# An f32 trunk of two layers on one core: the first feed-forward stage of layer 1 in parts of 8, 8 and 6 rows, and the S5 tables moved

## The chip, the cores and the metric

The kernel runs on 1 core of one Trainium2 chip. The time is device microseconds of one execution; lower is better. Before the change it was 1966.65 us (median of 3 runs, 1965.75 to 1967.88).

## The reference

The input `x` is 512 tokens of 1024 floats. Two layers follow, then a last RMSNorm. Each layer is a macaron:

```python
for i in range(DEPTH):                        # DEPTH = 2
    x = x + 0.5 * swiglu(rmsnorm(x, ffn1_norm[i]), ffn1_w_in[i], ffn1_w_out[i])
    h = rmsnorm(x, mix_norm[i])
    x = x + (ssd_mixer(h, ...) if i == 0 else s5_mixer(h, ...))
    x = x + 0.5 * swiglu(rmsnorm(x, ffn2_norm[i]), ffn2_w_in[i], ffn2_w_out[i])
return rmsnorm(x, final_norm)

def swiglu(h, w_in, w_out):                   # w_in 1024 x 5632, w_out 2816 x 1024
    gate, up = jnp.split(h @ w_in, 2, axis=-1)
    return (jax.nn.silu(gate) * up) @ w_out
```

The S5 mixer is a diagonal state-space model. The kernel computes it by turning inputs and states through tables of cosines and sines (eight tables of 128 x 2 x 8 x 64 floats, `s5["t"]`), which are made from the parameters and kept in DRAM.

## The kernel before

**Stages.** The program runs `f1_0`, `ssd`, `f2_0`, `f1_1`, `s5`, `f2_1` in this order; `f1` and `f2` are the two feed-forward stages of a layer, the last figure is the layer. All data is transposed: features on the 128 partitions, the 512 tokens along the free dimension (`xT[d]`, 8 tiles).

**A feed-forward stage** (`ffn`, L789). Its 2816 inner features are 22 rows of 128. A row is one gate and one up projection over 1024 inputs, then SiLU and product. The rows go in parts (L22 `PARTS`: 8, 7, 7; L23 `LAST_PARTS`: 8, 8, 6). After each part its rows are multiplied with their slice of `w_out` into the 8 output tiles, the columns `d`, and added to `xT`. Precision is kept by splitting every operand into a high and a low fp32r half (`whi` by ScalarE, `wlo` by VectorE) and adding three products: high x high, high x low, low x high.

**Two ways to multiply.** *Plain* (`proj`, L385): 128 x 128 weights against all 512 tokens. *Block products* (class `Seven`, L394): two by two blocks by a Strassen-Winograd scheme, seven products instead of eight. A row is two column blocks of the weights, split also into pairs of input tiles, and the tokens are split in halves of 256; so a product is 4 pairs x 3 matmuls of 256 tokens (`prod`, L464), and a row has 7 x 4 x 3 = 84 of them. VectorE and the accumulating DMAs from GpSimd (L407, L408) form the sums of weights.

Rows are block products in `f1_1` and `f2_1`, and from the fourth row on in `f2_0`. The output of a part is block products only where its end `b` is at most `blocks` (L822): then `seven_in` (L604) goes on behind the last row with `Columns` (L511), two columns of `w_out` at a time, so that rows, columns and the next part's rows are one unbroken sequence on TensorE. `Acts` (L533) forms the sums of the activations that this takes, during the rows. Before, `f1_1` is called with `blocks` 8 (first part alone) and `f2_1` with 16 (first and second part). Other outputs are plain (L888 to L930): for each column, load (`fetch_w`, L369), split (`split_w`, L378: cast at L380, low at L382), 3 matmuls for each row of the part (L389 to L391), evict.

**What sets the order.** TensorE's order in these stages is the program's (`manual_schedule`). VectorE's and ScalarE's instructions marked `pin` keep the program's order among themselves; the rest, and the DMA queues of SyncE (SP) and ScalarE, are ordered by the framework's scheduler, which often puts a load ahead of its place when its buffer is free. Every queue then runs in order. Weights pass through 4 buffers (`wst`), 3 of `whi` and 3 of `wlo`.

**Work threaded in: `fill`.** `ffn` calls one entry of the list `fill` after each row (not behind the first row of a part, where no row precedes) and after each plain output column (`pop`, L797). An entry issues foreign work at that place. Three kinds matter:

- *Angles* (`s5_angles`, L1587): VectorE computes cosines and sines in six pieces, in `f2_0` at entries 8 to 13, the plain output of its first part. They are stored in DRAM (`d_a`) for later.
- *Tables* (`s5_table`, L1632): each table call `i` makes two of the eight tables, for `i` and `i + 4`. It doubles the length of a complex power table six times (w = 1 to 32), by three VectorE operations each (L1653 to L1657, issued by the helper at L1637): 18 in all, on 128 x 16 w elements. Then four stores of 256 KB go out, issued by ScalarE (L1662). In three pieces (cut at operations 12 and 16). Calls 0 and 1 stand in `f2_0` at entries 23 to 28 (plain output of its second part). Calls 2 and 3 (`s5_late_tables`, L1669, with the angles loaded back by SP at L1675) stand in `f1_1` at entries 14 to 19 (plain output of its second part).
- *Loads for S5* in `f1_1`'s last plain output (entries from `end` = 29): operators `opP` (L1734) and `opH` (L1714), inputs `U` (L1707), tables `tb` (L1721) and the first GLU weights (`res_w`, L1745). The pools for these tiles (`s5_pools`, L2359) are opened by `renew` (L809) when the last block-product columns are done. The tiles `tb` and the tables under construction share three buffers.

Of the kernel before, what the change touches and what calls it, by code (L numbers as in the profile page):

```python
# [13 lines left out]
OP = mybir.AluOpType  # L14
# [7 lines left out]
PARTS = ((0, 8), (8, 15), (15, 22))  # L22
LAST_PARTS = ((0, 8), (8, 16), (16, 22))  # L23
# [6 lines left out]
PLAIN = 3  # L30
WARM = (4, 8)
RAW = 6
STAGES = ["f1_0", "ssd", "f2_0", "f1_1", "s5", "f2_1"]


@with_exitstack
def trunk_kernel(ctx, tc, x, ffn1_norm, ffn1_w_in, ffn1_w_out, mix_norm, ffn2_norm, ffn2_w_in, ffn2_w_out,
# [3 lines left out]
    nc = tc.nc  # L41
# [97 lines left out]
    def both(*fs):  # L139
        return lambda: [f() for f in fs]  # L140
# [648 lines left out]
    def ffn(pr, w_in, w_out, nxt, fill=(), ready=(), done=(), gates=(), hp=None, tail=None, blocks=0, behind=None):  # L789

        fill, ready, done, gates = list(fill), list(ready), list(done), list(gates)
# [9 lines left out]
        with tc.tile_pool(name="ffn", bufs=2, side="right", reuse_waits="tile") as fp:  # L801
# [15 lines left out]
                        pools.append(own.enter_context(tc.tile_pool(name="acts3", bufs=2, side="right", reuse_waits="tile")))  # L817
                return f

            for a, b in LAST_PARTS if final else PARTS:  # L820
                AH, AL = [], []
                if b <= blocks:  # L822
                    acts = Acts(pr, w_out, a, b, fp)
# [468 lines left out]
    s5 = {}  # L1292
# [294 lines left out]
    def s5_angles(tp):  # L1587

        c, s = s5["turn"][:, 0], s5["turn"][:, 1]
        t, d1, den = [tp.tile([128, 64], F32, name="t_" + nm, bufs=1)[:, 0:32] for nm in ("t", "d", "n")]  # L1590
        pin = tc.keep_in_program_order

        def tt(o, a, b, op):
            pin(V.tensor_tensor(o, a, b, op=op))

        def usq(cc, ss):
            tt(t, cc, ss, OP.mult)
            tt(cc, cc, cc, OP.mult)
            tt(d1, ss, ss, OP.mult)
            tt(den, cc, d1, OP.add)  # L1600
            tt(cc, cc, d1, OP.subtract)
            pin(V.tensor_scalar(den, den, -1.0, 2.0, op0=OP.mult, op1=OP.add))
            tt(cc, cc, den, OP.mult)
            pin(V.scalar_tensor_tensor(ss, t, 2.0, den, op0=OP.mult, op1=OP.mult))

        UC = tp.tile([128, 6, 32], F32, name="t_UC", bufs=1)
        US = tp.tile([128, 2, 6, 32], F32, name="t_US", bufs=1)

        def angles():
            usq(c, s)  # L1610
            usq(c, s)
            yield
            usq(c, s)
            for j in range(6):
                pin(V.tensor_copy(UC[:, j], c))
                pin(V.tensor_scalar(US[:, 0, j], s, -1.0, None, op0=OP.mult))
                pin(V.tensor_copy(US[:, 1, j], s))
                if j < 5:
                    usq(c, s)
                if j < 4:  # L1620
                    yield
            s5["a"] = dram.tile([128, 3, 6, 32], F32, name="d_a")
            nc.scalar.dma_start(s5["a"][:, 0], UC)
            nc.scalar.dma_start(s5["a"][:, 1:3], US)
            yield

        gen = angles()
        n = lambda: next(gen)
        tile = lambda nm, shp: tp.tile(shp, F32, name="t_" + nm, bufs=2 if nm == "cs" else 1)
        return [n] * 6 + [n for i in range(2) for n in s5_table(i, tile, lambda: (UC, US))]  # L1630

    def s5_table(i, tile, ang):  # L1632

        pin = tc.keep_in_program_order

        def tt(o, a, b, op):
            pin(V.tensor_tensor(o, a, b, op=op))  # L1637

        def table():
            UC, US = ang()  # L1640
            gs = slice(i * 8, i * 8 + 8)
            cs, tb = tile("cs", [128, 2, 8, 64]), tile("tb", [128, 2, 8, 32])
            pin(V.memset(cs[:, 0, :, 0:1], 1.0))
            pin(V.memset(cs[:, 1, :, 0:1], 0.0))
            for j in range(6):
                w = 1 << j
                shp = [128, 2, 8, w]
                bR = UC[:, j, gs][:, None, :, None].to_broadcast(shp)
                bI = US[:, :, j, gs][:, :, :, None].to_broadcast(shp)
                a_ = cs[:, :, :, 0:w]  # L1650
                sw = bass.AP(tensor=cs.tensor, offset=cs.offset + 512, ap=[list(cs.ap[0]), [-512, 2], [64, 8], [1, w]])
                o, t_ = cs[:, :, :, w:2 * w], tb[:, :, :, 0:w]
                tt(o, a_, bR, OP.mult)  # L1653
                if j == 5:
                    yield
                tt(t_, sw, bI, OP.mult)
                tt(o, o, t_, OP.add)  # L1657
                if j == 3:
                    yield
            for h in range(2):  # L1660
                for e in range(2):
                    nc.scalar.dma_start(s5["t"][i + 4 * h][64 * e:64 * e + 64], cs[64 * h:64 * h + 64])  # L1662
            yield

        gen = table()
        n = lambda: next(gen)
        return [n] * 3

    def s5_late_tables():  # L1669
        ang = {}  # L1670

        def load():
            for nm, a, b in (("UC", 0, 1), ("US", 1, 3)):
                t_ = s5["op"].tile([128, b - a, 6, 32], F32, tag="U", name="t" + nm, bufs=4)
                nc.sync.dma_start(t_, s5["a"][:, a:b])  # L1675
                ang[nm] = t_
            ang["tb"] = s5["op"].tile([128, 2, 8, 32], F32, tag="U", name="ttb", bufs=4)

        def tile(nm, shp):
            return s5["op"].tile(shp, F32, tag="tb", name="tcs", bufs=3) if nm == "cs" else ang["tb"]  # L1680

        return [load] + [n for i in range(2, 4) for n in s5_table(i, tile, lambda: (ang["UC"][:, 0], ang["US"]))]

    def s5_sink(d, g):

# [629 lines left out]
    for i, s in enumerate(stages[:-1]):  # L2315
        pr, prep = prep, prep_for(stages[i + 1])
        nxt = prep
        if s == "ssd":
            with tc.manual_schedule(engines=MAN):
                ssd(pr, nxt)  # L2320
        elif s == "s5":
            with tc.manual_schedule(engines=MAN):
                s5_stage(pr, nxt)
            op_es.close()
        else:
            L = int(s[-1])
            wi, wo = (ffn1_w_in, ffn1_w_out) if s[:2] == "f1" else (ffn2_w_in, ffn2_w_out)
            if s in s5_pre[:1]:
                with ExitStack() as third:

                    def tail():
                        pre_es.close()
                        hx.append(third.enter_context(tc.tile_pool(name="hx0", bufs=6, reuse_waits="tile")))
                        return third.enter_context(tc.tile_pool(name="h10", bufs=2, reuse_waits="tile"))

                    ffn(pr, wi[L], wo[L], nxt, fill=pre0, ready=ready, done=done, gates=[first_gate], tail=tail)
                    hx.clear()
            elif s in s5_pre:
                hx.append(ctx.enter_context(tc.tile_pool(name="hx", bufs=6, reuse_waits="tile")))
                with tc.tile_pool(name="hx1", bufs=2) as hp, tc.tile_pool(name="tabs", bufs=1) as tp, \  # L2340
                        tc.manual_schedule(engines=MAN):
                    tabs, fill = s5_angles(tp), [lambda: None] * 46
                    for n in (*range(8, 14), *range(23, 29)):
                        fill[n] = tabs.pop(0)
                    ffn(pr, wi[L], wo[L], nxt, fill=fill, hp=hp)
            elif stages[i + 1] == "s5":
                fill, tabs, end = [lambda: None] * 37, s5_late_tables(), 29
                for n in (9, *range(14, 20)):
                    fill[n] = tabs.pop(0)
                for j in range(2):  # L2350
                    for h in range(2):
                        fill[end + 2 * h + j] = lambda j=j, h=h: out_ops(j, h)
                for j in range(2):
                    fill[end + 2 + 2 * j] = lambda j=j: [f(j) for f in (in_h, in_u, in_t)]
                fill[end + 6] = lambda: out_ops(2, 0)
                for j in range(2 * NR):
                    fill[end + 1 + 2 * j] = lambda j=j: res_w(j)

                def s5_pools():  # L2359
                    s5["op"] = op_es.enter_context(tc.tile_pool(name="s5op", bufs=2))  # L2360
                    s5["up"] = up_es.enter_context(tc.tile_pool(name="s5u", bufs=2))

                with tc.manual_schedule(engines=MAN):
                    ffn(pr, wi[L], wo[L], nxt, fill=fill, blocks=PARTS[0][1], behind=s5_pools)
                up_es.close()
            else:
                turns = [lambda: None] * 14
                turns += [both(*[lambda d=d: fin_turn(d) for d in ds]) for ds in ((0, 1), (2, 3), (4, 5), (6,), (7,))]
                with tc.manual_schedule(engines=MAN):
                    ffn(pr, wi[L], wo[L], nxt, fill=turns, blocks=LAST_PARTS[1][1], behind=fin_open)  # L2370
# [29 lines left out]
```

## Time and profile before

| | |
|---|---|
| median of 3 runs | 1966.65 us |
| profiled execution | 1966.96 us |
| its span (first to last instruction) | 1965.2 us |
| TensorE busy | 1950.6 us (99%) |
| VectorE busy | 1613.0 us (82%) |
| ScalarE busy | 1009.5 us (51%) |
| granted TensorE clock | 0.999 |
| DMA | 303.94 MB, mean 155 GB/s |

In the profile PE is TensorE's matmuls, PEld its weight loads, DVE VectorE, ACT ScalarE, POOL GpSimd, SP SyncE; a q behind the name (SPq, ACTq) is an instruction that issues a DMA from that queue. `L472` is line 472 of the kernel. A row of the order of time gives start and length in us, engine and line, the operation, what it writes and reads, how many were merged, and in brackets how long the engine was idle before and what released it. Matmuls overlap their neighbours, so the time that one costs is the distance between starts, not its own length. In `f1_1` the rows of the first part run from about 1153, its block-product columns from 1232, the rows of the second part from 1275, its plain output from 1334, the rows of the third part from 1380, and its plain output from 1444 to 1484.

### The profile page before, as it was taken

What the parts mean: (1) busy time and instruction counts of PE and PEld (TensorE: products, weight loads), DVE (VectorE), ACT (ScalarE), POOL (GpSimd) and SP (SyncE); (2) the same over time, 40 slices, a digit from 0 to 9 for tenths busy, and PEclk for the clock granted to TensorE, in tenths of its full rate; (3) what the DMA queues carried; (4) which work ended last, traced back from release to release, by engine and by line L of the source; (5) the groups of instructions that cost most, each with busy time, mean ns of one, the idle gap of its engine ahead of it and who ended that gap; (6) DMA issues with size and microseconds to landing.
All of it is one profiled execution on the core that took longest, in us unless ns stands there. A gap on an engine that the chain in (4) does not pass through costs nothing.

```text
span 1965.2 us, 34460 instructions
## 1 busy us (share of the span) xinstructions
PE 1950.6 (99%) x13365; PEld 1758.1 (89%) x13365; DVE 1613.0 (82%) x2762; ACT 1009.5 (51%) x1611; POOL 286.0 (15%) x291
## 2 busy tenths in 40 slices
PE   9999999999999999999999999999999999999998
PEld 7888899888888888898989999998998889999997
DVE  7988878688888678877888899987878669989986
ACT  5323445465665355552535566452566446556463
POOL 1000011012111110110202112220201212222220
PEclk9999999999999999999999999999999999999999
DMA  8358767334333432684868669886987548888972
GB/s 201 100 151 204 181 145 164 100 113 142 108 107 113 115 89 72 136 182 114 183 152 185 159 135 184 188 185 170 201 255 229 165 99 169 181 183 184 192 161 86
DMA packets 535683, 303.94 MB, mean 155 GB/s; under 512 B 48896, under 2 KB 521120, under 8 KB 535520
## 3 DMA queue, kind: packets, MB, share of 16 engines
q1 hardware_dynamic: 428800, 224.66, 41.2%
q0 software_dynamic: 92640, 61.05, 20.7%
q10 hardware_dynamic: 14080, 16.04, 2.7%
q8 instruction: 105, 1.72, 0.4%
q14 instruction: 58, 0.48, 0.1%
HBM read 279.84 MB, written 21.33 MB: 153 GB/s over the span
## 4 chain that ended last, share of the span: by engine, by line
PE 94%; DVE 4%; issue 1%; ACT 1%; DMA 0%; ACTq 0%; DVEq 0%
PE mm L472 41%; PE mm L389 15%; PE mm L390 15%; PE mm L391 15%; PE aux L1203 1%; PE aux L1891 1%; PE aux L1145 1%; DVE wlo L426 1%; PE aux L1195 0%; PE aux L1096 0%; PE aux L389 0%; PE aux L390 0%; PE aux L391 0%; PE aux L1127 0%; PE aux L182 0%
## 5 line engine op out<-in xcount | busy, mean ns | idle before, releaser
L380 ACT CAST whi<-wst 128x1024 fp32r<-128x1024 f32 (+2 forms) x182 | 178.2, 984 | 294.6 <-PE mm L390 176.8
L472 PE MATMUL mm<-hx,whi 128*128 128x256 f32 x1680 | 312.1, 283 | 0.3 <-ACT gt L486 0.3
L426 DVE TENSOR_TENSOR wlo<-wst,whi 128x1024 fp32r<-128x1024 f32 x158 | 193.4, 1224 | 89.1 <-ACT whi L423 85.3
L472 PEld LDWEIGHTS mm<-hx,whi 128*128 128x128 f32 x1680 | 262.4, 192 | 1.0 <-ACT gt L486 0.5
L389 PE MATMUL mm<-hH,whi 128*128 128x512 f32 x664 | 263.3, 397 | 0.0
L391 PE MATMUL mm<-hH,wlo 128*128 128x512 f32 x664 | 259.0, 390 | 0.0
L390 PE MATMUL mm<-hL,whi 128*128 128x512 f32 x664 | 258.9, 390 | 0.0
L472 PE MATMUL mm<-hx,wlo 128*128 128x256 f32 x840 | 237.8, 283 | 0.2 <-DVE wlo L426 0.2
L382 DVE TENSOR_TENSOR wlo<-wst,whi 128x1024 fp32r<-128x1024 f32 (+2 forms) x182 | 207.2, 1141 | 29.7 <-ACT whi L380 27.9
L472 PE MATMUL mm<-hH,wlo 128*128 128x256 f32 x728 | 206.7, 284 | 0.7 <-DVE wlo L426 0.5
L472 PE MATMUL mm<-hL,whi 128*128 128x256 f32 x728 | 206.2, 283 | 0.5 <-DVE hL L273 0.3
L472 PE MATMUL mm<-hH,whi 128*128 128x256 f32 x728 | 206.1, 283 | 0.0
L423 ACT CAST whi<-wst 128x1024 fp32r<-128x1024 f32 x158 | 165.0, 1045 | 41.2 <-PE mm L472 11.7
L389 PE MATMUL mm<-ah,whi 128*128 128x512 f32 x464 | 180.7, 390 | 0.0
L390 PE MATMUL mm<-al,whi 128*128 128x512 f32 x464 | 180.6, 390 | 0.0
L391 PE MATMUL mm<-ah,wlo 128*128 128x512 f32 x464 | 180.2, 389 | 0.0
L408 POOL DMA_DIRECT2D wx<-in_ffn_w_in_dram x70 | 90.0, 1302 | 521.8 <-DMA wx<-in_ffn_w_in_dram 172.0
L472 PEld LDWEIGHTS mm<-hx,wlo 128*128 128x128 f32 x840 | 161.2, 192 | 0.4 <-DVE wlo L426 0.4
L407 POOL DMA_DIRECT2D wst<-in_ffn_w_in_dram x70 | 90.0, 1286 | 474.3 <-DMA d_P<-p_ks 196.3
L391 PEld LDWEIGHTS mm<-hH,wlo 128*128 128x128 f32 x664 | 124.6, 188 | 26.6 <-issue 0.2
L389 PEld LDWEIGHTS mm<-hH,whi 128*128 128x128 f32 x664 | 124.7, 188 | 25.8 <-issue 0.9
L390 PEld LDWEIGHTS mm<-hL,whi 128*128 128x128 f32 x664 | 124.8, 188 | 25.0 <-issue 0.2
(565 smaller groups left out, 4669.5 us busy)
## 6 DMA issues: line engine op xcount, KB each, us to landing
wst<-in_ffn_w_in_dram SPq DMA_DIRECT2D x175, 512.0 KB, 4.7
wst<-in_ssd_in_proj_dram SPq DMA_DIRECT2D x48, 512.0 KB, 3.9
wst<-in_ffn_w_out_dram SPq DMA_DIRECT2D x46, 512.0 KB, 4.2
wst<-in_ffn_w_out_dram SPq DMA_DIRECT2D x48, 448.0 KB, 4.5
wst<-in_ffn_w_in_dram POOLq DMA_DIRECT2D x70, 256.0 KB, 5.4
wx<-in_ffn_w_in_dram SPq DMA_DIRECT2D x70, 256.0 KB, 3.5
wx<-in_ffn_w_in_dram POOLq DMA_DIRECT2D x70, 256.0 KB, 6.2
dec<-d_cs POOLq DMA_DIRECT2D x16, 512.0 KB, 5.3
```

The source lines that it names most:

```text
L380: S.copy(hi, st)
L382: V.tensor_tensor(lo, st, hi.bitcast(F32), op=OP.subtract)
L389: PE.matmul(ps, hi[:, k], H[k], start=first and k == 0, stop=False)
L390: PE.matmul(ps, hi[:, k], L[k], start=False, stop=False)
L391: PE.matmul(ps, lo[:, k], H[k], start=False, stop=last and k == n - 1)
L407: G.dma_start(self.half(self.wu, 0), uo, accum_op=OP.add)
L408: G.dma_start(self.x[:, 0], ue, accum_op=OP.add)
L423: self.pin(S.copy(hi, st))
L426: self.pin(V.tensor_tensor(lo[:, c], st[:, c], hi[:, c].bitcast(F32), op=OP.subtract))
L472: PE.matmul(ps, w_[:, j], b_, start=nm not in self.open, stop=False, skip_group_check=True)
L1145: PE.matmul(pst[c], st["bt"][:, c * 128:(c + 1) * 128], st["wx"][:, c], start=True, stop=True)
L1203: PE.matmul(py[e][hh * 64:(hh + 1) * 64, s], st["dtx"][:, c, k0:k0 + 64], M[:, hh, s], start=True, stop=True)
```

## The change

- `f1_1` uses `LAST_PARTS` (8, 8, 6) and is called with `blocks` 16: its second part has 8 rows and its output is block products, its third part has 6 rows with plain output. `fill` shrinks from 37 entries to 28, and its last output column pass begins at `end` = 20 instead of 29. The last stage already used these parts.
- Table call 0 of `f2_0` moves to entries 16 to 21, behind rows of its second part, and is cut in six pieces (behind operations 6, 10, 13, 15, 16 and at the end), its stores behind the last. Calls 1 and 2, in three pieces each, take entries 23 to 28. `f2_0` so makes three table calls instead of two.
- Call 3 alone stays in `f1_1`: five pieces at entries 14 to 18, behind rows of the third part, the sixth at entry 20 (first plain output column), and its four stores at entry 27 (last column), issued by SP. The angles are loaded back when `s5_pools` opens the pools, now after the columns of the second part.

```diff
+SMALL = (6, 10, 13, 15, 16)
...
-            for a, b in LAST_PARTS if final else PARTS:
+            for a, b in LAST_PARTS if blocks else PARTS:
...
-        return [n] * 6 + [n for i in range(2) for n in s5_table(i, tile, lambda: (UC, US))]
-
-    def s5_table(i, tile, ang):
+        return [n] * 6 + [n for i in range(3) for n in s5_table(i, tile, lambda: (UC, US), *[SMALL][:i < 1])]
+
+    def s5_table(i, tile, ang, cuts=(12, 16), store=None):
...
-                tt(o, a_, bR, OP.mult)
-                if j == 5:
-                    yield
-                tt(t_, sw, bI, OP.mult)
-                tt(o, o, t_, OP.add)
-                if j == 3:
-                    yield
+                for k, (d_, x, y, op) in enumerate(((o, a_, bR, OP.mult), (t_, sw, bI, OP.mult), (o, o, t_, OP.add))):
+                    tt(d_, x, y, op)
+                    if 3 * j + k + 1 in cuts:
+                        yield
+            if store:
+                yield
             for h in range(2):
                 for e in range(2):
-                    nc.scalar.dma_start(s5["t"][i + 4 * h][64 * e:64 * e + 64], cs[64 * h:64 * h + 64])
+                    (store or nc.scalar).dma_start(s5["t"][i + 4 * h][64 * e:64 * e + 64], cs[64 * h:64 * h + 64])
             yield
...
-        return [n] * 3
+        return [n] * (len(cuts) + 1 + bool(store))
...
-        return [load] + [n for i in range(2, 4) for n in s5_table(i, tile, lambda: (ang["UC"][:, 0], ang["US"]))]
+        return [load] + s5_table(3, tile, lambda: (ang["UC"][:, 0], ang["US"]), SMALL, nc.sync)
...
-                    for n in (*range(8, 14), *range(23, 29)):
+                    for n in (*range(8, 14), *range(16, 22), *range(23, 29)):
                         fill[n] = tabs.pop(0)
...
-                fill, tabs, end = [lambda: None] * 37, s5_late_tables(), 29
-                for n in (9, *range(14, 20)):
+                fill, tabs, end = [lambda: None] * 28, s5_late_tables(), 20
+                load_angles = tabs.pop(0)
+                for n in range(14, 19):
                     fill[n] = tabs.pop(0)
...
+                fill[end] = both(tabs.pop(0), fill[end])
+                fill[end + 7] = both(fill[end + 7], tabs.pop(0))
 
                 def s5_pools():
...
+                    load_angles()
 
                 with tc.manual_schedule(engines=MAN):
-                    ffn(pr, wi[L], wo[L], nxt, fill=fill, blocks=PARTS[0][1], behind=s5_pools)
+                    ffn(pr, wi[L], wo[L], nxt, fill=fill, blocks=LAST_PARTS[1][1], behind=s5_pools)
```

## The prediction

> **What bounds the kernel now.** I read the page first, then busy time by stretch, then the chain and single engines' order of time inside the stage that changes (`f1_1`).
>
> ```profile
> span 1965.2 us, 34460 instructions
> ...
> PE   1950.6 (99%) x13365; PEld 1758.1 (89%) x13365; DVE 1613.0 (82%) x2762; ACT 1009.5 (51%) x1611; POOL 286.0 (15%) x291
> ```
>
> TensorE is busy 99% of the span: the program ends when the matmuls are done. The time can fall only by matmul time or by PE's waits, and rise only by new waits. The same by stretch (after the length: PE, PEld, DVE, ACT, POOL with counts, PE clock, DMA share, GB/s):
>
> ```profile
> 930.00:980.00 50.00, 50.00 (x419) 50.00 (x418) 40.85 (x60) 29.64 (x45) 12.83 (x10) 1.00 0.90 185
> ...
> 1334.00:1380.00 46.00, 45.47 (x227) 38.48 (x226) 35.28 (x75) 11.15 (x14) 2.56 (x2) 1.00 0.72 179
> 1380.00:1444.00 64.00, 64.00 (x534) 64.00 (x533) 54.74 (x81) 37.77 (x58) 12.84 (x10) 1.00 0.87 192
> 1444.00:1454.00 10.00, 10.00 (x53) 8.51 (x52) 6.38 (x10) 3.29 (x5) 0.00 (x0) 1.00 1.09 351
> 1454.00:1484.00 30.00, 30.00 (x136) 24.85 (x135) 17.73 (x26) 21.20 (x27) 0.71 (x2) 1.00 0.80 234
> ...
> 1755.00:1865.00 110.00, 110.00 (x919) 110.00 (x918) 101.29 (x160) 63.08 (x101) 28.27 (x22) 1.00 0.90 187
> ```
>
> The first is rows of `f2_0`'s second part. Then `f1_1`: plain output of its second part (1334 to 1380, the only stretch with PE short of full), rows of the third part (to 1444), plain output of the third part, which I call the tail (to 1484). The last is `f2_1`'s second part, rows and block-product columns: the code that the change gives to `f1_1`. PE is full there for all 110 us with DVE at 92% and DMA at 0.90, so the block path feeds PE without waits. The clock is 1.00 throughout.
>
> **The change part by part.** *Matmul time.* How far apart do matmuls start? Chain, a run of 256-column block products; and from PE's order of time the first matmul of output column 2 and the last of column 7 in the tail:
>
> ```profile
> 1152.88 181.43 PE mm L472 x1512
> ```
>
> ```profile
> 1455.09 0.39 PE L389 MATMUL mm<-ah,whi 128*128 128x512 f32 x1
> ```
>
> ```profile
> 1483.42 0.40 PE L391 MATMUL mm<-ah,wlo 128*128 128x512 f32 x1
> ```
>
> 181.43/1512 is 0.120 us for 256 columns. The other two are 6 columns x 7 rows x 3 = 126 matmuls, 125 intervals: 28.33/125 = 0.2266 us for 512 columns. So half the columns cost 53%, and seven products for eight give 7/8 x 2 x 0.120/0.2266 = 93%, not 87.5%.
> - Second part, plain, 7 rows: 7 x 8 x 3 = 168 x 0.2266 = 38.1 us go.
> - Second part, block, 8 rows: 4 column pairs x 7 products x 4 pairs of rows x 3 = 336 x 0.120 = 40.3 us come.
> - Third part, 6 rows for 7: 24 x 0.2266 = 5.4 us go.
>
> All 22 rows keep their 84 matmuls. Sum: -3.2 us. By the Trainium skill (TensorE: Matmul & The Clock Gate, "Wait — 56ns, not 53.3ns?") a warm matmul takes N ÷ 2.4 GHz and 2.5 ns, 109 and 216 ns; by it the sum would be an estimated -4.7 us. The rows disagree with it for both sizes (120 and 227 ns), and they decide.
>
> *PE's waits at the seam of second and third part.* PE, then ACT:
>
> ```profile
> 1376.47 0.28 PE L472 MATMUL mm<-hH,wlo 128*128 128x256 f32 x1
> 1377.00 0.51 PE L472 MATMUL mm<-hx,whi 128*128 128x256 f32 x2 [0.26 <-ACT gt L486]
> ```
>
> ```profile
> 1378.66 0.28 PE L472 MATMUL mm<-hL,whi 128*128 128x256 f32 x1
> 1379.21 0.39 PE L472 MATMUL mm<-hH,wlo 128*128 128x256 f32 x1 [0.27 <-DVE wlo L426]
> ```
>
> ```profile
> 1372.56 3.98 ACTq L1662 DMA_DIRECT2D d_t<-tcs  x4
> 1376.58 0.37 ACT L486 COPY gt<-mm 128x256 f32<-128x256 f32 x1 [6.55 <-DMA d_t<-tcs]
> ```
>
> Starts 0.53 and 0.55 us apart instead of 0.12: 0.84 us lost. ACT issues the four stores of a table for 3.98 us and reads the PSUM bank only then, so PE waits, and `wlo` is late behind it. The change puts no table there and joins the parts through the columns, as `f2_1` does with PE full. This stall goes: -0.8. What is late next there? Nothing in the 110 us of the twin; I keep 0 to 0.5 us of doubt. Together -4.0 us: that is the whole gain on offer.
>
> *A table among matrix rows.* Three groups of DVE's table arithmetic (two tables together, 1343 to 1379), then DVE's idle place in a row of `f1_1` and of `f2_0`, then ACT in the last row of `f2_0`'s second part:
>
> ```profile
> L1637 DVE TENSOR_TENSOR tcs<-tcs,ttb 128x16 f32<-128x16 f32 (+5 forms) x12 | 4.0, 334 | 0.2
> L1637 DVE TENSOR_TENSOR tcs<-tcs,tUC 128x16 f32<-128x16 f32 (+5 forms) x12 | 4.0, 332 | 0.2
> L1637 DVE TENSOR_TENSOR ttb<-tcs,tUS 128x16 f32<-128x16 f32 (+5 forms) x12 | 3.9, 329 | 0.0
> ```
>
> ```profile
> 1402.29 1.23 DVE L426 TENSOR_TENSOR wlo<-wst,whi 128x1024 fp32r<-128x1024 f32 x1 [1.09 <-ACT whi L423]
> ```
>
> ```profile
> 982.24 1.23 DVE L426 TENSOR_TENSOR wlo<-wst,whi 128x1024 fp32r<-128x1024 f32 x1 [1.68 <-ACT whi L423]
> ```
>
> ```profile
> 992.33 0.94 ACT L380 CAST whi<-wst 128x896 fp32r<-128x896 f32 x1 [0.98 <-PE mm L472]
> 995.81 0.63 ACT L500 ACTIVATE gt<-gt 128x512 f32<-128x512 f32 x1 [2.54 <-DVE gt L499]
> ```
>
> A table is 11.9/2 = 6.0 us of DVE in 18 operations, cut into six pieces: about 1 us a row on average. Behind a piece on DVE's queue stand the low half of the q4 weights and the next row's sum, then the `wlo` of the rows above, which waits for ACT anyway, 1.68 us in `f2_0` and 1.09 us in `f1_1`. A piece of 1.0 us fits under that, so I take 0; one 0.3 us too long in each of five rows without that cover would be 1.5 us. In `f2_0`'s last row ACT issues four stores (3.98 us by the row above) and has 0.98 + 2.54 = 3.5 us idle before the Silu. What stands behind them is the cast of output column 1, which PE wants only after column 0 (18 x 0.2266) and a product (12 x 0.120), 5.5 us. I take 0; without that cover it is 0.5 us.
>
> *The tail.* It shrinks from 168 x 0.2266 + 1.4 = 39.5 to 144 x 0.2266 + 1.4 = 34.1 us, so the weights must be ready sooner. Casts and lows of columns 3 (first of the pairs) and 7, and PE's starts (the second matmul of column 3, the first of column 7):
>
> ```profile
> 1456.09 1.78 ACT L380 CAST whi<-wst 128x896 fp32r<-128x896 f32 x2
> ```
>
> ```profile
> 1473.61 0.93 ACT L380 CAST whi<-wst 128x896 fp32r<-128x896 f32 x1
> ```
>
> ```profile
> 1458.10 2.08 DVE L382 TENSOR_TENSOR wlo<-wst,whi 128x896 fp32r<-128x896 f32 x2
> ...
> 1474.57 1.09 DVE L382 TENSOR_TENSOR wlo<-wst,whi 128x896 fp32r<-128x896 f32 x1 [0.97 <-ACT whi L380]
> ```
>
> ```profile
> 1460.08 0.39 PE L390 MATMUL mm<-al,whi 128*128 128x512 f32 x1
> ```
>
> ```profile
> 1478.89 0.39 PE L389 MATMUL mm<-ah,whi 128*128 128x512 f32 x1
> ```
>
> `wlo` of column 3 is ready at about 1459.1, wanted as third matmul at 1460.3: 1.2 us to spare. Column 7: ready 1475.66, wanted 1479.34: 3.7 us. Each row less takes 3 x 0.2266 = 0.68 us off every column before: three for column 3 (-2.0 us), seven for column 7 (-4.8 us). With unchanged ready times column 3 is 0.8 and column 7 1.1 us late, and the first wait covers most of the second: 1.1 us. Now the transfers of the tail, and where the tables' stores and reads lay:
>
> ```profile
> DMA packets 15733, 10.53 MB, mean 263 GB/s; under 512 B 6127, under 2 KB 14075, under 8 KB 15731
> ...
> wst<-in_ffn_w_out_dram SPq DMA_DIRECT2D x4, 448.0 KB, 7.5
> ```
>
> ```profile
> d_t<-tcs ACTq DMA_DIRECT2D x8, 256.0 KB, 4.6
> tb<-d_t SPq DMA_DIRECT2D x2, 512.0 KB, 5.1
> ```
>
> ```profile
> 1371.74 0.34 SPq L1721 DMA_DIRECT2D tb<-d_t  x1
> ```
>
> Stores (1 MB a table) and table reads (0.5 MB each) now fall between 1344 and 1384, where DMA was 0.72 busy. After the change the last table's stores stand on SP at the last column, and the read that reuses their buffer follows them. The pool that holds these tiles opens only in the third part, so the other two reads and the angles (0.3 MB by their shapes) go into its rows, which have 0.13 of DMA time free over 64 us; that holds 1.3 MB (7 us at 192 GB/s). Behind the stores on SP's queue stand S5's first reads of `d_u`; S5 takes the tables in turn, the third after two whole turns, so that costs nothing unless the transfers themselves are late. In the tail: 8 x 64 KB less weights (-0.5), +1.0 and +0.5: 11.5 MB in 34.1 us is 338 GB/s. The fullest 10 us (351) could do that, the tail's mean (263) could not. If only the net +0.5 MB of stores and weights stands ahead of the last weights, at 330 GB/s, that is 1.6 us more: 2.7 us lateness in all. I take the middle of 1.1 and 2.7: +1.9 us.
>
> Sum: -3.2 - 0.8 + 1.9 = -2.1 us. The profiled execution was 1966.96 us, 1.8 us around its span and 0.3 over the median of 1966.65, to which I apply the sum: **1964.5 us**.
>
> **The rivals.**
> 1. *All of the gain arrives* (-4.0 and up to 0.5 more from restarts after the two stalls: 1962.4). It needs the tail's weights to come earlier than in the old order. For it: the rows up to 1444 leave 0.13 of DMA time free and could start them; `f2_1` has no stall in its rows. Against: 1.2 us to spare at column 3.
> 2. *The tail stays as long as its data* (39.5 us): 5.4 us of waits, -4.0 + 5.4 = +1.4, 1968.1. For it: DMA at 1.09 in its first 10 us. Against: over its other 30 us DMA is at 0.80.
> 3. *Transfers moved into the tail make it DMA-bound: slower.* At the old mean of 263 GB/s 11.5 MB take 43.7 us, 9.6 us over 34.1: +5.6, 1972.3. It is slower by over 0.2% if the tail runs under 11.5 MB/(34.1 + 7.9 us) = 274 GB/s. For it: every store and read goes through the 16 engines that also bring the weights. Against: that mean holds 30 us at 234 GB/s in which DMA was not full (0.80). By the Trainium skill (Trainium Kernel Development and Optimization, "Key Constraints") transfers issued from SP, ACT and POOL share the same 16 engines and another issuer saves only issue time; that is this rival's ground, and the trace so far agrees only in that ACT's own 3.98 us go.
>
> That the change does something else than it says can be left out: `f2_1` runs the same loop.
>
> **How the numbers follow.** About 0.2% (3.9 us) is what a measurement here can tell from no change. My forecast (between -0.5 and -3.9) has 0.45, rival 1 0.27, rival 2 0.14, rival 3 0.14. Only rival 1 is faster by over 0.2%: 0.27; forecast and rival 2 are within: 0.59; rival 3 slower: 0.14. The range runs from 1961.6 (rival 1 with its doubt) to 1970.0 (half of rival 3's loss); what is left out is the outer half of rival 3 and a little below. The likeliest case alone: 1962.8 to 1966.2.
>
> **What the changed profile would show.** Right: 168 fewer + 24 fewer plain matmuls and 336 more block products in `f1_1`; no PE wait at the seam of second and third part, no table stores on ACT there; PE full in `f2_0`'s second part; the tail some 36 us long with waits for `wlo` or `whi` of columns 3 and 7. Wrong: PE short of full in `f2_0`'s rows or in the third part's rows (pieces too long, reads too many), a tail of 34 us without waits (rival 1), of 39 us or more (rivals 2 and 3), or S5's first turn waiting for a table.

## The result and the profile after

The changed kernel took 1978.43 us (median of 6 runs, 1977.25 to 1981.17); the kernel before, 1967.01 (6 runs, 1965.75 to 1968.29). The ratio is 1.0059 [1.0046, 1.0071]: 11.4 us slower, where 2 us faster was forecast, and outside the range. The profiled execution of the changed kernel took 1981.17 us, its span is 14.0 us longer than that of before. It is the longest of the six: the mean granted clock is 0.995 in it and in the next (1978.95 us), and 0.996 to 0.997 in the other four, so less of them ran at the slow clock that is shown below. The sums from this trace are therefore larger than the difference of the medians. Medians here are of all runs; the ratios leave out three runs of the last series that took 2204 us or more, one of them of the experiment with one more cut alone.

The page after:

```profile
span 1979.2 us, 34886 instructions
...
PE 1953.9 (99%) x13509; PEld 1767.7 (89%) x13509; DVE 1641.1 (83%) x2816; ACT 1022.5 (52%) x1642; POOL 296.4 (15%) x299
...
L473 PE MATMUL mm<-hx,whi 128*128 128x256 f32 x1680 | 313.4, 284 | 6.8 <-ACT gt L489 6.8
```

There are 144 more matmuls, as worked out (336 - 192). PE is still busy 99%: 7 us of idle do not show in a share. They show in the last column of the group: 6.8 us of waiting for one ScalarE copy, L489; before, this group waited 0.3 in all. (Lines up to about L1640 have moved by one: L472 is now L473.) By stretch, first the place where PE is short, last the rows of `f2_0` that the prediction showed:

```profile
985.00:990.00 5.00, 5.00 (x44) 5.00 (x44) 4.73 (x7) 3.99 (x6) 0.00 (x0) 1.00 0.44 86
990.00:995.00 5.00, 0.98 (x9) 0.77 (x7) 2.63 (x5) 0.05 (x1) 1.28 (x1) 0.85 0.92 227
995.00:1000.00 5.00, 2.26 (x10) 2.26 (x11) 0.00 (x0) 0.66 (x2) 0.00 (x0) 0.50 1.12 254
1000.00:1005.00 5.00, 5.00 (x24) 4.66 (x23) 2.89 (x4) 1.16 (x2) 0.00 (x0) 0.63 0.34 112
930.00:980.00 50.00, 50.00 (x419) 50.00 (x418) 44.28 (x77) 29.60 (x45) 12.82 (x10) 1.00 0.90 185
```

PE works 0.98 of 5 us, then 2.26, from there on at a clock of 0.50 to 0.63 (third figure from the end). This is `f2_0`'s last row before the plain output. ScalarE's order of time there, before and after:

```profile
989.38 0.62 ACT L423 CAST wh<-wst 128x512 fp32r<-128x512 f32 x1
989.89 0.37 ACT L488 COPY gt<-mm 128x256 f32<-128x256 f32 x1
990.96 0.38 ACT L491 ACTIVATE up<-mm 128x256 f32<-128x256 f32 x1 [0.70 <-PE mm L472]
```

```profile
989.43 0.61 ACT L424 CAST wh<-wst 128x512 fp32r<-128x512 f32 x1
992.09 5.19 ACTq L1662 DMA_DIRECT2D d_t<-t_cs  x4
997.32 0.37 ACT L489 COPY gt<-mm 128x256 f32<-128x256 f32 x1 [7.27 <-issue]
997.59 0.39 ACT L492 ACTIVATE up<-mm 128x256 f32<-128x256 f32 x1
1000.55 0.94 ACT L381 CAST whi<-wst 128x896 fp32r<-128x896 f32 x1 [2.57 <-PE mm L473]
```

After the cast of `wh` the copy came at once. Now the four stores of the table stand between them. VectorE's and PE's order of time after:

```profile
990.65 0.68 DVE L1638 TENSOR_TENSOR t_tb<-t_cs,t_US 128x512 f32<-128x512 f32 x1
991.37 0.69 DVE L1638 TENSOR_TENSOR t_cs<-t_cs,t_tb 128x512 f32<-128x512 f32 x1
991.98 0.68 DVE L427 TENSOR_TENSOR wl<-wst,wh 128x512 fp32r<-128x512 f32 x1
```

```profile
990.70 0.28 PE L473 MATMUL mm<-h,wlo 128*128 128x256 f32 x1
997.74 0.80 PE L473 MATMUL mm<-hx,whi 128*128 128x256 f32 x2 [6.76 <-ACT gt L489]
998.34 0.41 PE L473 MATMUL mm<-hx,wlo 128*128 128x256 f32 x1
998.55 0.63 PE L473 MATMUL mm<-hx,whi 128*128 128x256 f32 x2
998.98 0.41 PE L473 MATMUL mm<-hx,wlo 128*128 128x256 f32 x1
```

This reads as one sum. PE's next matmul was due at 990.82 (0.12 behind the last one) and starts at 997.74, 6.9 us late: 1.3 until the table's last operation ends (992.06) and the stores may start, 5.2 for their issue, 0.4 for the copy. Then the matmuls are 0.215 us apart (998.55 to 998.98 holds two) instead of 0.120: in the trace the granted clock is 0.5 from 993.5 us for 10.2 us, so 6.0 us of work run at that pace after the idle time, which loses 6.0 x (1 - 0.120/0.215) = 2.7. Together 9.6; from 995 to 1037 us of the old trace, each matmul comes 9.7 us later than there.

Following one matmul against its twin in the old trace through the rest of the program gives the whole 14.0:

| place | us against before |
|---|---|
| `f2_0`, last row of the second part and what follows it | +9.8 |
| `f1_1`, from 1280 to the end of its tail | -2.1 |
| opening of S5 (3.9 of it by the first matmul of L1805) | +6.3 |

In sum, `f1_1` did what was forecast. Its stretches (second part's columns, third part's rows, start and rest of the tail):

```profile
1340.00:1386.00 46.00, 46.00 (x385) 46.00 (x385) 42.73 (x70) 25.55 (x43) 12.44 (x10) 1.00 0.87 180
1386.00:1452.00 66.00, 65.62 (x546) 65.41 (x545) 62.15 (x104) 36.79 (x57) 13.23 (x11) 1.00 0.89 199
1452.00:1462.00 10.00, 10.00 (x67) 9.18 (x67) 7.96 (x14) 4.46 (x9) 0.00 (x0) 1.00 0.91 287
1462.00:1492.00 30.00, 29.20 (x131) 23.65 (x130) 18.64 (x28) 19.47 (x27) 1.20 (x2) 1.00 0.92 274
```

and PE's waits from 1275 to 1492 as the list of waits has them:

```profile
PE mm L392 <- DVE wlo L383: 0.8, 1, 0.8
PE mm L473 <- DVE wlo L427: 0.4, 1, 0.4
```

The first is column 3 of the tail. ScalarE's casts of columns 3 and 4 (the second row) stood behind the cast of the second GLU weight tile, for whose transfer it waited (the old kernel waited 3.80 us for the same tile):

```profile
1467.82 1.14 ACT L1752 CAST hH<-wst 128x512 fp32r<-128x512 f32 x2 [5.41 <-DMA wst<-in_s_glu_w_dram]
1468.86 1.57 ACT L381 CAST whi<-wst 128x768 fp32r<-128x768 f32 x2
```

The opening of S5, PE's order of time:

```profile
1492.97 0.43 PE L183 MATMUL aux<-ones,acc 128*32 128x1 f32 x32 [0.56 <-DVE acc L217]
1495.51 0.70 PE L183 MATMUL aux<-ones,sq 128*32 128x1 f32 x32 [2.10 <-ACT sq L210]
```

### The profile page after: what moved, and what is told of

It is laid out like the page before. It is cut to its first block, busy times and chain, and to the rows that moved or that the text cites. A ratio compares the mean times of both kernels' runs of the same rounds, so it can differ in the third digit from the quotient of the medians.

```text
span 1979.2 us, 34886 instructions
## 1 busy us (share of the span) xinstructions
PE 1953.9 (99%) x13509; PEld 1767.7 (89%) x13509; DVE 1641.1 (83%) x2816; ACT 1022.5 (52%) x1642; POOL 296.4 (15%) x299
## 4 chain that ended last, share of the span: by engine, by line
PE 92%; DVE 4%; ACT 2%; DMA 1%; issue 1%; ACTq 0%; SPq 0%; DVEq 0%
PE mm L473 41%; PE mm L390 14%; PE mm L391 14%; PE mm L392 14%; PE aux L1204 1%; PE aux L1891 1%; DVE wlo L427 1%; PE aux L1146 1%; PE aux L1196 0%; DMA opP<-d_P 0%; ACTq L1662 0%; PE aux L1097 0%; PE aux L390 0%; PE aux L391 0%; PE aux L392 0%
## 5 line engine op out<-in xcount | busy, mean ns | idle before, releaser
L473 PE MATMUL mm<-hx,whi 128*128 128x256 f32 x1680 | 313.4, 284 | 6.8 <-ACT gt L489 6.8
L381 ACT CAST whi<-wst 128x1024 fp32r<-128x1024 f32 (+3 forms) x174 | 169.9, 981 | 274.2 <-PE mm L391 174.8
L473 PEld LDWEIGHTS mm<-hx,whi 128*128 128x128 f32 x1680 | 263.3, 193 | 7.5 <-ACT gt L489 7.0
L427 DVE TENSOR_TENSOR wlo<-wst,whi 128x1024 fp32r<-128x1024 f32 x164 | 200.7, 1224 | 76.2 <-ACT whi L424 72.2
L473 PE MATMUL mm<-hx,wlo 128*128 128x256 f32 x840 | 238.6, 284 | 0.2 <-DVE wlo L427 0.2
L383 DVE TENSOR_TENSOR wlo<-wst,whi 128x1024 fp32r<-128x1024 f32 (+3 forms) x174 | 197.8, 1140 | 30.1 <-ACT whi L381 28.2
L473 PE MATMUL mm<-hH,wlo 128*128 128x256 f32 x728 | 206.9, 284 | 0.8 <-DVE wlo L427 0.6
L473 PE MATMUL mm<-hL,whi 128*128 128x256 f32 x728 | 206.4, 283 | 0.5 <-DVE hL L274 0.3
L473 PE MATMUL mm<-hH,whi 128*128 128x256 f32 x728 | 206.3, 283 | 0.0
L424 ACT CAST whi<-wst 128x1024 fp32r<-128x1024 f32 x164 | 171.2, 1044 | 40.6 <-PE mm L473 15.6
L473 PEld LDWEIGHTS mm<-hx,wlo 128*128 128x128 f32 x840 | 161.8, 193 | 0.4 <-DVE wlo L427 0.4
L392 PE MATMUL mm<-ah,wlo 128*128 128x512 f32 x400 | 155.5, 390 | 0.8 <-DVE wlo L383 0.8
L390 PE MATMUL mm<-ah,whi 128*128 128x512 f32 x400 | 156.3, 391 | 0.0
L391 PE MATMUL mm<-al,whi 128*128 128x512 f32 x400 | 155.9, 390 | 0.0
```

The source lines that it names most:

```text
L381: S.copy(hi, st)
L383: V.tensor_tensor(lo, st, hi.bitcast(F32), op=OP.subtract)
L390: PE.matmul(ps, hi[:, k], H[k], start=first and k == 0, stop=False)
L391: PE.matmul(ps, hi[:, k], L[k], start=False, stop=False)
L392: PE.matmul(ps, lo[:, k], H[k], start=False, stop=last and k == n - 1)
L424: self.pin(S.copy(hi, st))
```

## The experiments

The theory (T1): ScalarE's queue order costs the time. The scheduler put call 0's four stores, which must wait for VectorE's last piece, in front of the copy that frees the PSUM bank of PE's next product. The rivals: the table's arithmetic or its 1 MB among matrix rows is what costs (and would cost from any queue or place), or (T2) call 3's stores in the tail cost a large share through what they do to S5's opening, 4 to 6 us of the 11.4. Times are medians; "before" is the old kernel beside it in the same series (1966.61, 1966.81 and 1967.04 us).

**Call 0's stores from SP**, at the same place, nothing else changed:

```diff
-        return [n] * 6 + [n for i in range(3) for n in s5_table(i, tile, lambda: (UC, US), *[SMALL][:i < 1])]
+        return [n] * 6 + [n for i in range(3) for n in s5_table(i, tile, lambda: (UC, US), *((SMALL, nc.sync) if i < 1 else ()))]
...
-                        fill[n] = tabs.pop(0)
+                        fill[n] = both(tabs.pop(0), tabs.pop(0)) if n == 21 else tabs.pop(0)
```

> The changed kernel with one edit: the four stores of table call 0 in f2_0 are issued by SP instead of ScalarE, at the same place. Theory (ScalarE's stores stand in front of the PSUM copy that the next block product waits for; the 7 us idle time then halves PE's clock for a while): both losses of f2_0, 7.0 and 2.6 us, go; time 1968.8 us, between 1967.5 and 1970, PE full from 985 to 1005. Rival (the six pieces of the table on VectorE, or the 1 MB of transfers, hold up f2_0's last row): the pieces and bytes are unchanged, so the stall of some 7 us stays and the time stays at 1977 to 1979.

1966.72 us (10 runs), ratio 1.0000 [0.999, 1.0009]: 11.7 us below the changed kernel, and below the expected 1967.5 to 1970, which had kept the whole loss at S5's opening. The same two stretches and the copy:

```profile
990.00:995.00 5.00, 4.94 (x40) 4.69 (x40) 4.61 (x7) 2.32 (x5) 1.28 (x1) 1.00 0.81 218
995.00:1000.00 5.00, 5.00 (x29) 4.32 (x27) 1.42 (x3) 0.63 (x1) 0.00 (x0) 1.00 1.04 237
```

```profile
990.63 0.36 ACT L489 COPY gt<-mm 128x256 f32<-128x256 f32 x1
```

PE is all but full (9.94 of 10 us) at clock 1.00, with the same arithmetic, the same bytes and the DMA engines nearly as busy (0.81 and 1.04 against 0.92 and 1.12). Pieces and bytes are out as causes of the stall.

**Call 0's stores still from ScalarE, one entry later** (its stores become an entry of their own, number 22):

```diff
+        return [n] * 6 + [n for i in range(3) for n in s5_table(i, tile, lambda: (UC, US), *((SMALL, nc.scalar) if i < 1 else ()))]
...
-                    for n in (*range(8, 14), *range(16, 22), *range(23, 29)):
+                    for n in (*range(8, 14), *range(16, 29)):
```

> The changed kernel with the four stores of call 0 still on ScalarE but one entry later, behind the two PSUM copies and one weight cast. Theory (it is what stands behind them in the queue, not which engine issues): no stall at the copy, time 1968.8 us (1967.5 to 1971, since the Silu of the last row now stands behind 3 to 5 us of stores and may cost up to 1.5 us). Rival (ScalarE can't issue these stores in a row stage without harm): a stall of 3 us or more remains near the end of that part, time over 1973.

1967.92 us (10 runs), 1.0006 [0.9997, 1.0016]. ScalarE's order of time:

```profile
989.80 0.36 ACT L489 COPY gt<-mm 128x256 f32<-128x256 f32 x1
990.87 0.38 ACT L492 ACTIVATE up<-mm 128x256 f32<-128x256 f32 x1 [0.70 <-PE mm L473]
992.24 0.94 ACT L381 CAST whi<-wst 128x896 fp32r<-128x896 f32 x1 [0.98 <-PE mm L473]
992.26 5.62 ACTq L1662 DMA_DIRECT2D d_t<-t_cs  x4
997.98 0.63 ACT L501 ACTIVATE gt<-gt 128x512 f32<-128x512 f32 x1 [4.80 <-issue]
```

The issue is even longer (5.62), on the same engine, and PE does not wait: the copies, and a cast, are ahead of it. So it is not ScalarE as issuer but what stands behind the issue. This is close to the place that the prediction had reasoned about (there the cast stood behind the stores).

**Call 3 moved to `f2_0` too**, to rows of its third part, from SP; no table work in `f1_1`:

```diff
-        return [n] * 6 + [n for i in range(3) for n in s5_table(i, tile, lambda: (UC, US), *[SMALL][:i < 1])]
+        return [n] * 6 + [n for i in range(4) for n in s5_table(i, tile, lambda: (UC, US), *((SMALL, nc.sync) if i in (0, 3) else ()))]
...
-                    for n in (*range(8, 14), *range(16, 22), *range(23, 29)):
-                        fill[n] = tabs.pop(0)
+                    for n in (*range(8, 14), *range(16, 22), *range(23, 29), *range(31, 37)):
+                        fill[n] = both(tabs.pop(0), tabs.pop(0)) if n in (21, 36) else tabs.pop(0)
...
-                load_angles = tabs.pop(0)
-                for n in range(14, 19):
-                    fill[n] = tabs.pop(0)
...
-                fill[end] = both(tabs.pop(0), fill[end])
-                fill[end + 7] = both(fill[end + 7], tabs.pop(0))
...
-                    load_angles()
```

> As e1, and call 3 moves out of f1_1 altogether: its six pieces go behind the rows of f2_0's third part, its stores by SP there. f1_1 keeps 8, 8, 6 with no table work in it. Theory T2 (the 1 MB of stores on SP in the tail delays the last GLU weights, ScalarE waits for them in front of the squares that end the stage, and S5 starts late): S5 starts without the 3 us idle time and without the slow clock behind it; 4 to 6 us less than e1, 1963 to 1965 us, below the kernel before. Rival R2 (six rows give the tail 5.4 us less, and ScalarE's and the transfers' work for S5 does not fit, whoever stores): within 1.5 us of e1, 1967 to 1969.

1965.71 us (10 runs), 0.9996 [0.9986, 1.0005]: 1.0 below the first experiment, not 4 to 6. T2's size falls. Its mechanism does not: see the end of the list.

**The old parts with all tables in `f2_0`** (the third experiment with parts of 8, 7, 7 rows):

```diff
-            for a, b in LAST_PARTS if blocks else PARTS:
+            for a, b in LAST_PARTS if final else PARTS:
...
-                fill, tabs, end = [lambda: None] * 28, s5_late_tables(), 20
+                fill, tabs, end = [lambda: None] * 37, s5_late_tables(), 29
...
-                    ffn(pr, wi[L], wo[L], nxt, fill=fill, blocks=LAST_PARTS[1][1], behind=s5_pools)
+                    ffn(pr, wi[L], wo[L], nxt, fill=fill, blocks=PARTS[0][1], behind=s5_pools)
```

> As e3 but f1_1 in the old parts 8, 7, 7 with only the first as block products: what the tables' new places are worth by themselves, and against e3 what the parts are worth. Theory: the kernel before without the 1.0 us seam stall, 1965.5 to 1966.5; e3 is lower by up to 3 us. Rival R2: e4 is lower than e3 by 1 us or more.

1968.12 us (10 runs), 1.0008 [0.9999, 1.0018], above the expected 1965.5 to 1966.5; why is open (its profiled execution took 1966.74). The third experiment is 2.4 us below it by the medians: that is what the new parts are worth when nothing disturbs them. Twins in the two traces give about 1.5 for the stretch from 1153 us to the end of the tail. Here the seam has no stall either, since no table stands there.

**Two of call 0's four stores on SP, two left on ScalarE** in front of the copy:

```diff
-                    (store or nc.scalar).dma_start(s5["t"][i + 4 * h][64 * e:64 * e + 64], cs[64 * h:64 * h + 64])
+                    (store or (nc.sync if i == 0 and h else nc.scalar)).dma_start(s5["t"][i + 4 * h][64 * e:64 * e + 64], cs[64 * h:64 * h + 64])
```

> The changed kernel with two of the four stores of call 0 left on ScalarE at their place in front of the PSUM copy, the other two on SP. Theory (the idle time is DVE's lead plus what ScalarE needs to issue the stores, 5.2 us for four): two take some 1.2 to 2.6 us, so PE idles 2.5 to 4 us instead of 6.9. If the clock drop needs an idle time longer than that, the granted clock stays at 1.0 there and the 2.6 us behind the wait go too: 1970 to 1971 us; else 1972 to 1973. Rival (one blocked instruction costs the same however many stores stand before it): as the changed kernel, 1977 to 1979.

1972.35 us (6 runs), 1.0029 [1.0018, 1.004]. ScalarE and the stretch after the wait:

```profile
992.55 1.17 ACTq L1662 DMA_DIRECT2D d_t<-t_cs  x2
993.76 0.37 ACT L489 COPY gt<-mm 128x256 f32<-128x256 f32 x1 [3.26 <-DVE wl L427]
```

```profile
990.00:995.00 5.00, 2.24 (x18) 2.04 (x18) 3.08 (x5) 1.16 (x3) 1.28 (x1) 1.00 0.89 231
995.00:1000.00 5.00, 5.00 (x26) 4.79 (x25) 2.71 (x4) 0.94 (x1) 0.00 (x0) 0.66 1.10 246
```

A dose between none and four: PE loses 2.9 us (due at 991.27, starts at 994.19), and the clock still falls, to 0.5 for 3.4 us from 995.4, after PE is back at work. Two stores issue in 1.17 us, not half of 5.19; 1.3 us of the wait is for VectorE's last operation, and 0.4 for the copy. The trace of the changed kernel shows why it is not half: one by one the four issues take 0.51, 0.60, 2.06 and 1.91 us. The first two are as cheap there; what holds the third and fourth is open.

**The table in `f2_0` alone**: the fourth experiment (old parts, nothing in `f1_1`), with call 0's stores on ScalarE in front of the copy:

```diff
-        return [n] * 6 + [n for i in range(4) for n in s5_table(i, tile, lambda: (UC, US), *((SMALL, nc.sync) if i in (0, 3) else ()))]
+        return [n] * 6 + [n for i in range(4) for n in s5_table(i, tile, lambda: (UC, US), *((SMALL, nc.sync if i else nc.scalar) if i in (0, 3) else ()))]
```

> As e4 (old parts 8, 7, 7 in f1_1, all table calls in f2_0) but call 0's stores on ScalarE in front of the PSUM copy, as in the changed kernel. Theory (the loss belongs to that place in f2_0 and needs nothing of f1_1's new parts): e4 plus 9 to 10 us, 1977 to 1978.5. Rival (the loss comes only together with f1_1's change): as e4.

1976.68 us (4 runs), 1.0052 [1.0038, 1.0065]: 8.6 above its base, a little under the 9 to 10 expected, with `f1_1` in the old parts and without tables. Stretches:

```profile
990.00:995.00 5.00, 1.94 (x17) 1.73 (x15) 3.59 (x5) 1.01 (x2) 1.28 (x1) 1.00 0.75 212
995.00:1000.00 5.00, 1.03 (x5) 1.03 (x6) 0.00 (x0) 0.66 (x2) 0.00 (x0) 0.70 1.09 175
```

**S5's operators behind the second GLU tile** (the third experiment; the tail's waits by another order of loads):

```diff
-                s5["last P"] = nc.sync.dma_start(P_, src)
+                with tc.issue_after(s5["glu 1"].ins) if "glu 1" in s5 else ExitStack():
+                    s5["last P"] = nc.sync.dma_start(P_, src)
...
-        nc.sync.dma_start(st, glu_cols(j).rearrange("(k p) c -> p k c", p=128))
+        s5[f"glu {j}"] = nc.sync.dma_start(st, glu_cols(j).rearrange("(k p) c -> p k c", p=128))
```

> As e3, with S5's operator loads (2 MB that the scheduler puts ahead of the second GLU weight tile in the tail) issued behind that tile. Theory (ScalarE's wait of 4.9 us for that tile, and PE's wait of 0.7 us at output column 3 behind it, come from those 2 MB and not from the six rows): ScalarE's wait falls below 2 us, PE's wait goes, 0.5 to 1 us less than e3, about 1965. Rival (the tail is short of transfer rate whatever the order): the wait moves to another tile, time as e3 or, if the operators now come late for S5, 1 to 3 us more.

1968.62 us (11 runs), 1.001 [1.0001, 1.0019]: 2.9 worse than its base, where 0.5 to 1 better was expected. ScalarE, then PE's waits:

```profile
1454.12 1.14 ACT L1753 CAST hH<-wst 128x512 fp32r<-128x512 f32 x2 [3.96 <-DMA wst<-in_s_glu_w_dram]
1455.17 0.83 ACT L381 CAST whi<-wst 128x768 fp32r<-128x768 f32 x1
1456.17 0.62 ACT L615 CAST ah<-up 128x512 fp32r<-128x512 f32 x1 [0.17 <-DVE up L510]
```

```profile
PE mm L390 <- ACT ah L615: 2.0, 1, 2.0
PE mm L391 <- DVE al L618: 0.9, 1, 0.9
```

It made the same fault a second time, in another place: the scheduler moved a cast that waits for a transfer in front of `ah`, which PE needs; the clock then was 0.5 for 3.4 us from 1458.8.

**One more cut in the small pieces** (behind operation 17 too, the last piece and the stores one entry later), first together with the order of loads above and then without it:

```diff
-SMALL = (6, 10, 13, 15, 16)
+SMALL = (6, 10, 13, 15, 16, 17)
...
-                    for n in (*range(8, 14), *range(16, 22), *range(23, 29), *range(31, 37)):
-                        fill[n] = both(tabs.pop(0), tabs.pop(0)) if n in (21, 36) else tabs.pop(0)
+                    for n in (*range(8, 14), *range(16, 29), *range(31, 38)):
+                        fill[n] = both(tabs.pop(0), tabs.pop(0)) if n in (22, 37) else tabs.pop(0)
```

> As e6, with the last piece of calls 0 and 3 cut once more: the 18th operation and the stores go behind the last row instead of in it. Theory (a piece of two operations, 1.3 us, is too long for the last row of a part, where the low half of the q4 weights stands behind it: 0.3 us of PE wait in the second part and 0.7 us in the third): both waits go, 0.6 to 1.0 us less than e6, about 1964. Rival: no change within 0.5 us.

> e3 with the last piece of calls 0 and 3 cut once more (18th operation and stores behind the last row), and the operator loads left where they were. Theory (e7 less e6 was the worth of the cut, 0.9 us, and the operators' new place was e6's loss): e3 less 0.9 us, 1964.5 to 1965.2, PE waits of 0.3 and 0.7 us gone in f2_0, nothing lost in the tail. Rival (the cut is worth nothing in the median): as e3, 1965.5 to 1966.5.

1967.7 us (11 runs), 1.0006 [0.9997, 1.0015], 0.9 below its base; without the order of loads 1964.66 us (12 runs), 0.9989 [0.998, 0.9998], 1.05 below the third experiment, though in another series. The last piece held two operations of 0.7 us, and in the third experiment the weights' low half behind it (`wl`, L427) made PE lose 0.3 us in the last row of `f2_0`'s second part and 0.65 in that of its third. With the cut both are gone, and twins in the two traces give the same 1.0 us for these rows. The longest wait left in `f1_1` is at column 3:

```profile
1460.25 0.50 PE L392 MATMUL mm<-ah,wlo 128*128 128x512 f32 x1 [0.59 <-DVE wlo L383]
```

**The second GLU tile one column later**, with that:

```diff
-                    fill[end + 1 + 2 * j] = lambda j=j: res_w(j)
+                    k = end + 1 + 2 * j + (j == 1)
+                    fill[k] = both(fill[k], lambda j=j: res_w(j)) if j == 1 else lambda j=j: res_w(j)
```

> e9 with the second GLU weight tile loaded and split one output column later, so that ScalarE has the casts of columns 3 and 4 in front of its wait for that tile. Theory (PE's last wait in the tail, 0.7 us at column 3, is ScalarE's order and not the transfer rate): that wait goes, e9 less 0.7 us, about 1964. Rival (the tail has no room: the tile then holds up the later squares and S5 starts later): PE's wait goes but the time stays or rises by up to 2 us.

1964.30 us (12 runs), 0.9987 [0.9979, 0.9996]. The wait at column 3 is gone, so that wait came from ScalarE's order; PE is busy 209.55 of 210 us from 1270 to 1480. Its lead over the version before (0.4) is within the scatter. This is the best version: 2.7 us below the kernel before, 14 below the change.

**S5's opening, over all traces.** The distance from the last matmul of the tail to the first `rm,qsel` matmul of S5 (L1805) is 4.13 us before and 4.12 to 4.42 in the seven experiments without table stores in the tail. In the four kernels with them it is 8.04 (the change), 4.81, 5.77 and 5.56 (first, second and fifth experiment). So call 3's work in `f1_1` does cost there, 0.7 to 3.9 us as the execution falls, and three of these four show a clock of 0.5 in that place as well (6.8, 3.4 and 3.4 us). Five of the seven have the short tail too, so it is not the six rows. No run takes the stores out alone; that they are the cause is read from SP's and ScalarE's order of time in the changed kernel:

```profile
1479.43 1.69 SPq L1662 DMA_DIRECT2D d_t<-tcs  x2
...
1482.57 2.20 SPq L1662 DMA_DIRECT2D d_t<-tcs  x1
```

```profile
1485.16 1.14 ACT L1752 CAST hH<-wst 128x512 fp32r<-128x512 f32 x2 [2.03 <-DMA wst<-in_s_glu_w_dram]
...
1493.48 1.15 ACT L1687 ACTIVATE s5u<-xT,cols 128x512 f32<-128x512 f32 x1 [1.29 <-DMA d_u<-s5u]
1495.04 0.72 ACT L210 ACTIVATE sq<-xT 128x256 f32<-128x256 f32 x2 [0.40 <-ACT s5u L1687]
```

The stores stand among the weights and inputs; ScalarE waits 2.03 us for the weights and 1.29 for a store of `d_u`, the squares for the norm come late, and PE waits 2.10 us for them. (The old trace has a wait of 1.98 us for such a tile as well, without harm: it ends 12 us before the tail's last matmul, here 6 us before.) What stays open is how often an execution pays the large price: the first and third experiment differ by 1.0 us in their medians, with overlapping intervals.

## Why the prediction was wrong

**The step that failed** is in "A table among matrix rows": "What stands behind them is the cast of output column 1, which PE wants only after column 0 [...] I take 0; without that cover it is 0.5 us." The stores were placed in thought behind the row's last copies, into idle time that the old trace showed (0.98 + 2.54 us). In the run they stood two instructions earlier, in front of those last copies (`gt`, `up`). What stood behind them was the copy of a PSUM bank that PE's next product overwrites: no cover at all. Worth 9.6 us in the trace by place, 8.6 in the experiment that has only this, 11.7 between the medians of the changed kernel and the first experiment. (The profiled executions of these two also differ by some 5 us at S5's opening; how much of the last figure that is in the medians is open.) The second experiment comes close to the prediction's picture, and there PE has no wait behind the stores: the step's 0 holds.

The old profile had the warning, and the prediction quoted it: at the seam of `f1_1` the same four stores stood in front of `ACT gt L486` for 3.98 us, and PE was late behind it. The prediction took that stall off and did not ask whether the same queue would make it again at the table's new place. Nor did it ask why the seam was cheap (0.84 us): there the issue began at 1372.56, 4 us before PE wanted the bank; here PE wanted it at 990.82 and the issue began at 992.09.

**The price of a wait was mis-sized too.** Even the stated bound without cover, 0.5 us, would have needed the issue time to be as before. It was 5.19 us here against 3.98 (DMA share 1.03 while it lasted, 0.89 at the seam), and idle time brought a slower clock behind it. The prediction read the clock of 1.00 throughout as a fact of before and did not ask on what it depends. By the Trainium skill (TensorE: Matmul & The Clock Gate, "What's actually happening") an idle window of about 3.4 us takes the clock to 4/8. The trace agrees with the size: 0.5, for 3.4, 6.8 or 10.2 us. It does not agree that a gap must be that long: 2.9 us of idle were enough in the fifth experiment.

**Right:** the sum for `f1_1`, and most of its terms. Matmul time -3.2, the stall at the seam gone, the tail late: net -2.1 forecast, -2.1 measured. That it agrees to the tenth is luck. The lateness was 1.2 us at column 3 alone (0.80 of it idle in the list of waits) against 1.9 taken; 0.3 and 0.65 were lost in rows where VectorE's low half was late, against a doubt of 0 to 0.5 that the sum left out; and the seam's stall was 1.05 with the restarts behind its two waits, not 0.84. The 0.8 of the 1.9 that the prediction took from the rate of the transfers is not borne out either: the last two kernels move the same bytes, and in the last the wait at column 3 is gone, since ScalarE's casts no longer stand behind the second GLU tile.

**Right in part:** "A piece of 1.0 us fits". PE was full from 930 to 980 with VectorE at 44.28 of 50 instead of 40.85. The last piece, two operations of 0.7 us, did not fit: 0.3 and 0.65 us lost in the third experiment, and one cut more was worth about 1 us.

**Wrong in the tail's transfers:** rival 3 (a tail bound by DMA) did not happen; PE had 29.20 of 30 us at 274 GB/s. But the sentence on S5 ("that costs nothing unless the transfers themselves are late") missed that PE's first matmuls of S5 hang on ScalarE, and ScalarE's order on a weight tile whose load stands between the stores. The prediction's list of what would show it wrong had "S5's first turn waiting for a table"; it waited for squares instead.

Without the fault the change would have been about no change: the first experiment is at 1.0000. In its profile the stretch from 1153 us to the end of the tail is 2.5 us shorter than before, of which 0.5 goes to waits in `f2_0`'s rows and 0.7 to S5's opening; the 1.3 that is left does not show in the medians. Differences of that size need many runs: up to 890 us, where all these kernels are the same, the profiled executions already lie between 0.9 us ahead of the old one and 1.3 behind it.

## What to carry to other kernels

When work with a DMA issue is moved, find the instruction that will stand behind the issue on that engine's queue, at the new place, for each position that the scheduler may choose; if it is a PSUM copy that TensorE waits for, whatever of the issue time falls behind the moment when TensorE wants the bank is on the path. Price an issue by the longest row seen, with room above it (3.98 us became 5.19 and 5.62 here), plus the wait for its data, plus the half clock that followed a gap of 2.9 us and more. From a queue with no compute behind it, or behind the copies, the same stores made no stall here (1.0000 and 1.0006 of the time before).

## What the hardware showed that was not expected

- Issue time from ScalarE is not a fixed price: four stores of 256 KB took 3.98 us at the seam (3.0 to 3.2 at the old kernel's three other places), 5.19 and 5.62 at the new one, two stores 1.17. The first two of four took 0.45 to 0.61 us each throughout; the differences are in the third and fourth. By the Trainium skill (Trainium Kernel Development and Optimization, "Key Constraints") issuing from several engines only saves the sequencer's issue time. The runs show no other saving, and here that time, in front of the wrong copy, was worth some 10 us.
- Within the program the half clock came in stretches of 3.4 us and their multiples, and not in proportion to the gap: 6.9 us of idle brought 10.2 us of it in the changed kernel, 7.2 us brought 6.8 in the experiment with the table alone (from 997.0), 2.9 us brought 3.4. At S5's opening, two gaps of 0.56 and 2.10 us among small matmuls were followed by 6.8 us.
